# Interleaving two arrays on one core: one DMA queue in a fixed order and 64 KiB store rows, in place of two queues and a graded tail

## The chip, the core and the metric

The kernel runs on one core of a Trainium2 chip. The time is that of the device for one execution, in microseconds. Of the kernel before, five executions were timed: a median of 318.57 us, from 318.37 to 319.57. One more view of it is a profile of a single execution, which took 318.37 us; its span, from the first to the last instruction, is 316.2 us. The remaining 2.17 us lie around the span.

## The reference

Two arrays of 32 x 256 x 1024 single-precision numbers are interleaved element by element. Nothing is calculated; the task is moving 67.11 MB in and 67.11 MB out.

```python
def reference(x, y):
    batch, seq, dim = x.shape
    result = np.zeros((batch, seq, dim * 2), dtype=np.float32)
    result[..., 0::2] = x
    result[..., 1::2] = y
    return result
```

Since the last dimension is interleaved and the arrays are contiguous, the output is the flat x and the flat y interleaved, whatever the outer dimensions are. The kernel treats all three arrays as flat.

## The kernel before

The on-chip memory has 128 partitions. A tile takes a contiguous piece of the flat x and of the flat y and lays it over the 128 partitions, so many columns on each. The list `lwidths` (line 39) holds the widths in columns: seven tiles of 8192, then a graded tail of 4096, 2048, 1024, 512 and 512. A tile of 8192 columns is 4.19 MB of x and as much of y.

For each tile (loop at line 43) two loads are issued by SyncE's queue (SP): x at line 49, y at line 50. The pools `xp` and `yp` have two buffers each of 128 x 8192, so the loads of one tile can run while the one before is in use. The DMA engines' queue of SP appears as q1 in the profile.

Inside a tile an inner loop (line 53) takes up to 4096 columns at a time. For each piece VectorE (DVE) makes two copies into an output buffer `otile`, x into the even columns (line 63) and y into the odd ones (line 64), and ScalarE's queue (ACT) issues the store (line 65). The output pool `op` has two buffers of 128 x 8192. A store of a full piece writes a row of 32 KiB for each partition, 4.19 MB in all. The DMA queue of ACT appears as q10.

No order is written out by hand beyond this: SP issues the loads in the order of the tiles, ACT the stores in the order of the pieces, and each instruction waits for the semaphores that its buffers need. A load waits until the copy has read what was in its buffer two tiles earlier; the first copy of a piece waits until the store two pieces earlier has landed; a store waits for its second copy. Loads and stores of the two queues run on the same 16 DMA engines. All copies run on DVE; the other engines compute nothing.

Of the kernel before, what the change touches and what calls it, by code (L numbers as in the profile page):

```python
# [2 lines left out]

# [4 lines left out]


@with_exitstack
def kernel(
    ctx: ExitStack,
    tc: tile.TileContext,
    x: bass.AP,
    y: bass.AP,
    out: bass.AP,
):
    nc = tc.nc
    P = 128  # L20

    total = 1
    for s in x.shape:
        total *= s

    WL = 8192
    WS = 4096

    xf = x.rearrange("b s d -> (b s d)")
    yf = y.rearrange("b s d -> (b s d)")  # L30
    of = out.rearrange("b s d -> (b s d)")

    fp32 = mybir.dt.float32

    xpool = ctx.enter_context(tc.tile_pool(name="xp", bufs=2))
    ypool = ctx.enter_context(tc.tile_pool(name="yp", bufs=2))
    opool = ctx.enter_context(tc.tile_pool(name="op", bufs=2))

    lwidths = [WL] * (total // P // WL - 1) + [4096, 2048, 1024, 512, 512]
    assert sum(lwidths) == total // P  # L40

    start = 0
    for lw in lwidths:
        xtile = xpool.tile([P, WL], fp32, name="xtile")[:, :lw]
        ytile = ypool.tile([P, WL], fp32, name="ytile")[:, :lw]

        xs = dataclasses.replace(xf, offset=start, ap=[[lw, P], [1, lw]])
        ys = dataclasses.replace(yf, offset=start, ap=[[lw, P], [1, lw]])
        nc.sync.dma_start(out=xtile, in_=xs)  # L49
        nc.sync.dma_start(out=ytile, in_=ys)  # L50

        soff = 0
        while soff < lw:
            width = min(WS, lw - soff)
            otile = opool.tile([P, 2 * WS], fp32, name="otile")[:, : 2 * width]
            os_ = dataclasses.replace(
                of,
                offset=2 * start + 2 * soff,
                ap=[[2 * lw, P], [1, 2 * width]],
            )  # L60
            xsub = xtile[:, soff : soff + width]
            ysub = ytile[:, soff : soff + width]
            nc.vector.tensor_copy(out=otile[:, 0::2], in_=xsub)  # L63
            nc.vector.tensor_copy(out=otile[:, 1::2], in_=ysub)  # L64
            nc.scalar.dma_start(out=os_, in_=otile)
            soff += width

        start += P * lw
    assert start == total


# [1 line left out]
_INS = ['x', 'y']  # L73
_OUTS = [((32, 256, 2048), 'float32')]


# [23 lines left out]
```

## Time and profile before

| | |
|---|---|
| median of five executions | 318.57 us |
| profiled execution, whole | 318.37 us |
| its span | 316.2 us |
| bytes moved, in and out | 134.22 MB |
| mean rate over the span | 424 GB/s |
| copies on VectorE | 38, 73.5 us busy |
| one copy of 128 x 4096 | 2.295 us |
| loads of 4096 KB, from issue to landing (median) | x 43.6 us, y 60.8 us |
| stores of 4096 KB, from issue to landing (median) | 29.1 us |

A time from issue to landing includes the time that a transfer stands behind others in its queue. Of the profile's views, the slices show how full the 16 DMA engines are over the span, the queues show what each of the two queues moved, the chain follows the work that ended last back from the end, and the stretches give the DMA rate between any two moments. The rate by stretches counts a packet where it starts, so a stretch of a microsecond or two swings above and below the mean; stretches of a whole tile don't.

### The profile page before, as it was taken

What the parts mean: (1) busy time and instruction counts of PE and PEld (TensorE: products, weight loads), DVE (VectorE), ACT (ScalarE), POOL (GpSimd) and SP (SyncE); (2) the same over time, 40 slices, a digit from 0 to 9 for tenths busy, and PEclk for the clock granted to TensorE, in tenths of its full rate; (3) what the DMA queues carried; (4) which work ended last, traced back from release to release, by engine and by line L of the source; (5) the groups of instructions that cost most, each with busy time, mean ns of one, the idle gap of its engine ahead of it and who ended that gap; (6) DMA issues with size and microseconds to landing.
All of it is one profiled execution on the core that took longest, in us unless ns stands there. A gap on an engine that the chain in (4) does not pass through costs nothing.

```text
span 316.2 us, 179 instructions
## 1 busy us (share of the span) xinstructions
DVE 73.5 (23%) x38; POOL 0.2 (0%) x4
## 2 busy tenths in 40 slices
DVE  0334002232022410325003150130502223221022
POOL 0000000000000000000000000000000000000000
DMA  8999999999999999999999999999999999999997
GB/s 332 406 456 390 406 464 398 464 410 452 423 439 431 431 431 431 452 410 456 406 460 402 464 402 460 423 439 427 435 431 431 439 444 404 433 460 423 396 417 299
DMA packets 6192, 134.22 MB, mean 424 GB/s; under 512 B 688, under 2 KB 688, under 8 KB 1712
## 3 DMA queue, kind: packets, MB, share of 16 engines
q1 hardware_dynamic: 3456, 67.11, 49.9%
q10 hardware_dynamic: 2736, 67.11, 49.2%
HBM read 67.11 MB, written 67.11 MB: 424 GB/s over the span
## 4 chain that ended last, share of the span: by engine, by line
DMA 76%; DVE 11%; another core or an unknown queue 10%; issue 0%; DVEq 0%; SPq 0%
DMA out_dram<-otile 63%; DMA ytile<-in_y_dram 13%; DVE otile L64 6%; DVE otile L63 5%; DVEq L63 0%; SPq L49 0%
## 5 line engine op out<-in xcount | busy, mean ns | idle before, releaser
L63 DVE COPY otile<-xtile 128x4096 f32<-128x4096 f32 (+3 forms) x19 | 37.1, 1958 | 193.7 <-DMA out_dram<-otile 170.7
L64 DVE COPY otile<-ytile 128x4096 f32<-128x4096 f32 (+3 forms) x19 | 37.1, 1955 | 45.4 <-DMA ytile<-in_y_dram 45.4
L84 POOL MEMSET const-bfloat16-1.0<- 128x1 bf16 x1 | 0.1, 101 | 0.0
L84 POOL MEMSET const-uint8-127<- 128x1 uint8 x1 | 0.1, 101 | 0.0
L84 POOL MEMSET const-float32-0.0<- 128x1 f32 x1 | 0.1, 98 | 0.2 <-issue 0.2
L84 POOL MEMSET const-float32-1.0<- 128x1 f32 x1 | 0.1, 98 | 0.0
## 6 DMA issues: line engine op xcount, KB each, us to landing
out_dram<-otile ACTq DMA_DIRECT2D x15, 4096.0 KB, 29.1
xtile<-in_x_dram SPq DMA_DIRECT2D x7, 4096.0 KB, 43.6
ytile<-in_y_dram SPq DMA_DIRECT2D x7, 4096.0 KB, 60.8
xtile<-in_x_dram SPq DMA_DIRECT2D x1, 2048.0 KB, 38.8
ytile<-in_y_dram SPq DMA_DIRECT2D x1, 2048.0 KB, 51.2
out_dram<-otile ACTq DMA_DIRECT2D x1, 2048.0 KB, 7.7
xtile<-in_x_dram SPq DMA_DIRECT2D x1, 1024.0 KB, 29.8
ytile<-in_y_dram SPq DMA_DIRECT2D x1, 1024.0 KB, 36.1
```

What stands on the lines that cost most here:

```text
L63: nc.vector.tensor_copy(out=otile[:, 0::2], in_=xsub)
L64: nc.vector.tensor_copy(out=otile[:, 1::2], in_=ysub)
L84: nc = _bacc.Bacc("TRN2", target_bir_lowering=False, num_devices=1)
```

## The change

The tail is no longer graded: the kernel now runs eight tiles of 8192 columns. All DMAs, stores too, are issued from SyncE's queue, in an order that the program writes out: loads of tiles 0 and 1; then, for each tile t, its copies and its store, and after it the loads of tile t + 2. The output pool has one buffer of 128 x 16384 instead of two of 128 x 8192, and a tile's copies and its store cover all its columns at once, so a store writes a row of 64 KiB for each partition. Only the last tile is split in two halves of 4096 columns, and its output goes through the buffers of the x and y pools that tile 6 has left free.

The same on-chip memory is used: 192 KiB of each partition in both kernels (four input buffers of 32 KiB, and 64 KiB for output).

```diff
-    lwidths = [WL] * (total // P // WL - 1) + [4096, 2048, 1024, 512, 512]
-    opool = ctx.enter_context(tc.tile_pool(name="op", bufs=2))
+    opool = ctx.enter_context(tc.tile_pool(name="op", bufs=1))
...
-        nc.sync.dma_start(out=xtile, in_=xs)
-        nc.sync.dma_start(out=ytile, in_=ys)
...
-            nc.vector.tensor_copy(out=otile[:, 0::2], in_=xsub)
-            nc.vector.tensor_copy(out=otile[:, 1::2], in_=ysub)
-            nc.scalar.dma_start(out=os_, in_=otile)
...
+    def load(t):
+        if t >= n:
+            return
+        base = t * P * W
+        xt = xpool.tile([P, W], fp32, name="xtile")
+        yt = ypool.tile([P, W], fp32, name="ytile")
+        for tl, src in ((xt, xf), (yt, yf)):
+            s = dataclasses.replace(src, offset=base, ap=[[W, P], [1, W]])
+            nc.sync.dma_start(out=tl, in_=s)
+        tiles[t] = (xt, yt)
+
+    def emit(t, off, width, ot):
+        xt, yt = tiles[t]
+        nc.vector.tensor_copy(out=ot[:, 0::2], in_=xt[:, off : off + width])
+        nc.vector.tensor_copy(out=ot[:, 1::2], in_=yt[:, off : off + width])
+        d = dataclasses.replace(
+            of, offset=2 * (t * P * W + off), ap=[[2 * W, P], [1, 2 * width]]
+        )
+        nc.sync.dma_start(out=d, in_=ot)
+
+    load(0)
+    load(1)
+    for t in range(n):
+        if t < n - 1:
+            ot = opool.tile([P, 2 * S], fp32, name="otile")
+            emit(t, 0, S, ot)
+        else:
+            for i, pool in enumerate((xpool, ypool)):
+                ot = pool.tile([P, W], fp32, name="xtile" if i == 0 else "ytile")
+                emit(t, i * W // 2, W // 2, ot)
+        load(t + 2)
```

Here n is 8, P is 128, and W and S are both 8192.

More of the change, by code (lines that the diff above doesn't have):

```diff
@@ L20 @@
     P = 128
+    W = 8192
+    S = 8192
     total = 1
@@ L24 @@
         total *= s
-    WL = 8192
-    WS = 4096
+    n = total // (P * W)
+    assert n * P * W == total
     xf = x.rearrange("b s d -> (b s d)")
@@ L36 @@
     ypool = ctx.enter_context(tc.tile_pool(name="yp", bufs=2))
-    opool = ctx.enter_context(tc.tile_pool(name="op", bufs=2))
-    lwidths = [WL] * (total // P // WL - 1) + [4096, 2048, 1024, 512, 512]
[L40 to L64, printed above, removed]
-            nc.scalar.dma_start(out=os_, in_=otile)
-            soff += width
-        start += P * lw
@@ L69 @@
-    assert start == total
+    opool = ctx.enter_context(tc.tile_pool(name="op", bufs=1))
+    tiles = {}
+    def load(t):
[16 more added lines that the diff above has]
+        nc.sync.dma_start(out=d, in_=ot)
```

## The prediction

> **What bounds the kernel now.** I read the page first: engines, then DMA queues, then the chain of waits; then the DMA rate by stretches, because the chain alone misleads here.
>
> ```profile
> DVE 73.5 (23%) x38; POOL 0.2 (0%) x4
> DMA packets 6192, 134.22 MB, mean 424 GB/s; under 512 B 688, under 2 KB 688, under 8 KB 1712
> q1 hardware_dynamic: 3456, 67.11, 49.9%
> q10 hardware_dynamic: 2736, 67.11, 49.2%
> DMA out_dram<-otile 63%; DMA ytile<-in_y_dram 13%; DVE otile L64 6%; DVE otile L63 5%; DVEq L63 0%; SPq L49 0%
> ```
>
> VectorE (DVE) works 23% of the span. The two queues (q1 loads, q10 stores) together fill 99.1% of the 16 DMA engines' time. So the chain's "stores 63%" and the 170.7 us in which DVE waits for stores name who waits, not what is scarce: while one store is late, the engines are moving something else. A cure for those waits alone is worth nothing. The stretches show where the engines are not full:
>
> ```profile
> 0.00:20.00 20.00, 4.50 (x2) 0.20 (x4) 1.00 0.95 393
> 20.00:40.00 20.00, 4.50 (x2) 0.00 (x0) 1.00 1.00 415
> 40.00:58.57 18.57, 4.59 (x2) 0.00 (x0) 1.00 0.99 429
> 58.57:97.31 38.74, 9.09 (x4) 0.00 (x0) 1.00 1.00 433
> 97.31:136.02 38.71, 9.09 (x4) 0.00 (x0) 1.00 1.00 433
> ...
> 281.30:302.86 21.56, 3.84 (x4) 0.00 (x0) 1.00 1.00 421
> 302.86:311.70 8.84, 0.76 (x2) 0.00 (x0) 1.00 0.98 407
> 311.70:316.20 4.50, 0.84 (x2) 0.00 (x0) 1.00 0.54 220
> ```
>
> The last two columns are the engines' busy share and GB/s. In the middle one tile of 8192 columns (8.39 MB in, 8.39 MB out) takes 38.73 us, 433.3 GB/s, five times over (58.57 to 252.21). At that rate 134.22 MB need 309.76 us of the 316.2. The other 6.4 us, each as length x (1 - rate/433.3): start 1.86; 20 to 40, where the first store enters, 0.85; 40 to 58.57 about 0.18; the graded tail 0.61 + 0.54 + 2.2 = 3.35; the rest small. Only these can be won.
>
> The same rate with loads alone: the first two loads of 4.19 MB, one queue, are seen to land when their copies start.
>
> ```profile
> 0.73 0.37 SPq L49 DMA_DIRECT2D xtile<-in_x_dram  x1
> 1.15 0.42 SPq L50 DMA_DIRECT2D ytile<-in_y_dram  x1
> 13.10 4.50 DVE L63 COPY otile<-xtile 128x4096 f32<-128x4096 f32 x2 [13.10 <-DMA xtile<-in_x_dram]
> 22.78 4.50 DVE L64 COPY otile<-ytile 128x4096 f32<-128x4096 f32 x2 [5.18 <-DMA ytile<-in_y_dram]
> ```
>
> 22.78 - 13.10 = 9.68 us for 4.19 MB, again 433 GB/s, with a completion between the two loads.
>
> **What the Trainium skill says.** The page "DMA: Bandwidth & Descriptors" bears on it four times. "Where 436 GB/s comes from" gives a ceiling of 435.2 GB/s for the core's 16 ports; the trace's 433.3 lies 0.4% under it, so the middle has nothing to give. "Issuing engines are not separate DMA queues" says that transfers from all issuing engines share the same 16 engines, so a second queue adds no bandwidth; one queue at 433 (start) and two at 433 (middle) agree. "Queues, rings and completion order" says an engine takes one ring's descriptors in order without barriers, only the semaphore increment waits for earlier writes; the load-to-load boundary above agrees, a store-to-load boundary inside one ring is in no part of this trace. "Why a DMA increments its semaphore by 16 and not by 1" has one descriptor move one contiguous run and names rows *longer* than 64 KiB as those to be cut, so I expect a 64 KiB row to stay whole; the trace has only rows up to 32 KiB.
>
> **The change, part by part.**
>
> *Copies.* 38 copies become 14 of 8192 columns and 4 of 4096. The 8192 form is not shown; from the rows of 4096 (2295 ns) and 2048 (1228 ns) a column costs 0.52 ns, so it takes 2295 + 4096 x 0.52 = 4.43 us (between 4.43 and twice 2295, 4.59). A tile costs 8.9 us, as before (9.09).
>
> *Single output buffer.* Copies of tile t+1 now wait for the whole store t, then need 8.9 us before store t+1 can be issued. What covers this is the load pair of tile t+2, queued right behind store t: 2 x 9.68 = 19.4 us. Slack 10.5 us, less a completion and an issue (a store's shortest issue-to-landing was 2.6 us): still some 8. Cost nothing. Without the cover it would be 8.9 plus about 2 us for each of six tiles, 65 us.
>
> *One queue on SP.* Store t waits on SP for the second copy; behind it wait only the loads of tile t+2. They were issued after their own buffer's copy and now go out about 4.4 us later for x, and one issue (0.33 us) later for y. At store 0 that is 22.78 + 4.43 = 27.2 us; the second pair keeps the engines busy until 13.10 + 3 x 9.68 = 42.1. Afterwards each store is issued about 8 us before the load pair in front of it ends. Nobody starves. ACT's queue has nothing left; POOL's had nothing.
>
> *Order of directions.* Before, both queues always held work, so reads and writes alternated packet by packet. Now 8.39 MB of stores alternate with 8.39 MB of loads: seven entries into stores, six back. Unseen: pure-store rate, and a switch inside one ring. Nearest row: the first store, 0.85 us lost once. Later a direction changed at nearly every packet at no loss, so I take the 0.85 as the price of the first store, paid once, and 0 for the other twelve; bounds 0 and 0.85 each.
>
> *Rows of 64 KiB.* Half as many store packets. A 32 KiB packet takes 16 x 32768 B / 433.3 GB/s = 1.210 us, 5 ns above the ceiling's 1.205. Stores are 128 such packets per engine, and 7/8 of them are paired: between 0 and 0.3 us gained. I take the middle, 0.15.
>
> *Tail.* The five graded tiles go; tile 7 is full. Its load pair stands before store 6 in the queue, its four copies (4 x 2.3 us; the first needs only x) and both stores fall under store 6's 19.4 us. The engines stay full to the last packet, in rows of 32 KiB. Only the landing and the closing barrier remain: the last store before was issued at 312.7, landed 2.6 us later, 315.3; to the end 0.9 us.
>
> *Sum.* Lead of the first load, 13.10 - 9.68 = 3.42; data 309.76; first store 0.85; end 0.9: span 314.9, that is 1.3 us less. The profiled execution took 318.37, 2.17 beyond its span: 317.1. It lies 0.2 under the median of 318.57, so the sum stated for a median is 317.3; less the packets' 0.15, I predict 317.1. It is a gain of 0.46%; 0.2%, 0.64 us, is about what can be told from no change: under 317.9 is faster, over 319.2 slower.
>
> **Rivals.**
>
> *A: a switch costs each time (slower).* Each entry of a store behind a load in one ring costs what the first store cost, because no second ring fills the gap. For it: the 415 GB/s stretch is the only time a store began with no store before it. Against: packetwise alternation cost nothing later. Price 6 more x 0.85 = 5.1: 322.2. From (319.2 - 317.1) / 6 = 0.35 us per entry on, the kernel is slower.
>
> *B: stores alone run below loads alone.* For it: no pure-store stretch is seen. Against: q10's share for equal bytes is smaller (49.2 to 49.9%). At 425 GB/s the stores take 157.9 instead of 154.9 us: 320.1. Slower below 427.5.
>
> *C: a little of both, no change.* A completion's wait inside the ring, 0.1 us at each of 13 switches, gives 1.3 us: 318.4, between 317.9 and 319.2.
>
> *D: the tail's gain is whole and pure phases reach the ceiling.* First store free (0.85), and the stores' half of the data at 435.2 (0.7, the packets' gain within it) in place of the 0.15: 317.1 - 0.85 - 0.55 = 315.7 at best.
>
> **How the numbers follow.** Forecast, with its own range 316.2 to 317.9: 0.44; D below it 0.08; C 0.17; A 0.17; B 0.10; something unseen that lets the queue run dry 0.04. Faster 0.44 + 0.08 = 0.52; same 0.17; slower 0.31. The range leaves out about one in ten on each side: 315.9 cuts the end of D, 321.9 keeps A up to 0.8 us per entry and cuts its full price and the dry queue.
>
> **What would show it.** Right: copies of 4.4 us; each store issued before the load pair ahead of it ends; 433 GB/s in store stretches and across switches; full slices to the last; 128 packets a store besides the completions; span near 314.9. Wrong: a dip at each switch (A), stores of 8.39 MB spaced over 19.5 us (B), DVE's second copy ending after the load pair has landed (dry queue).

## The result: no difference that matters, and one late DMA engine

The changed kernel took 318.76 us (median of 43 executions, 317.05 to 319.66); the kernel before, beside it, 319.0 us (80 executions). The ratio is 0.9988, with a 95% interval of 0.9981 to 0.9995: the kernel is faster by 0.12%, where 0.46% was forecast. Its profiled execution took 319.21 us and has a span of 317.4, not 314.9. Beyond the span lie 1.78 us; in the kernel before it was 2.17.

The page of the changed kernel, its lines on engines, DMA packets, the queue, and the chain by line:

```profile
DVE 70.4 (22%) x18; POOL 0.2 (0%) x4
DMA packets 3600, 134.22 MB, mean 423 GB/s; under 512 B 400, under 2 KB 400, under 8 KB 400
q1 hardware_dynamic: 3600, 134.22, 98.4%
...
DMA out_dram<-otile 49%; DMA ytile<-in_y_dram 22%; DVE otile L56 8%; DVE otile L55 7%; DVE xtile L56 1%; DVEq L99 1%; SPq L50 0%; SPq L60 0%; DVEq L55 0%
```

3600 packets are 25 DMAs of 128 rows and 16 completions each, so a row of 64 KiB travels as one packet. The queue fills 98.4% of the engines' time; before, two queues filled 99.1%. Nothing on this page says what is wrong. The stretches do. The columns are again the busy share of the DMA engines and GB/s at the end of each line:

```profile
20.00:40.00 20.00, 4.43 (x1) 0.00 (x0) 1.00 0.99 419
62.62:101.50 38.88, 8.77 (x3) 0.00 (x0) 1.00 1.01 437
101.50:140.46 38.96, 8.77 (x3) 0.00 (x0) 1.00 1.00 432
140.46:179.83 39.37, 8.76 (x3) 0.00 (x0) 1.00 1.00 431
179.83:219.61 39.78, 8.76 (x2) 0.00 (x0) 1.00 1.00 433
...
297.30:311.00 13.70, 0.00 (x0) 0.00 (x0) 1.00 1.01 438
311.00:313.00 2.00, 0.00 (x0) 0.00 (x0) 1.00 0.83 360
313.00:315.00 2.00, 0.00 (x0) 0.00 (x0) 1.00 0.04 16
315.00:317.40 2.40, 0.00 (x0) 0.00 (x0) 1.00 0.03 14
```

The rate holds at 431 to 437 through every change of direction, as forecast. But a tile, bounded here by the moments when a whole store has landed, takes 38.9 us at first and up to 39.8, against 38.73. And the end is odd: from 313 to 317.4 the 16 engines are 3 to 4% busy. One sixteenth is 6%, so on average less than one engine is still at work there while all the others are done. Such an end is called a foot below.

The trace also records when each of the 16 engines has landed its share of a DMA. It doesn't name the engine, so first, median and last below are those of each DMA by itself. For the second load of some tiles and for the last store (us; the last column is the distance between the first and the last engine):

```
changed kernel                first    median   last     spread
y of tile 0                    22.05    22.42    22.68    0.63
y of tile 1                    42.26    42.61    43.04    0.79
y of tile 3                   119.72   120.15   120.91    1.19
y of tile 4                   158.43   158.88   160.39    1.96
y of tile 5                   197.13   197.62   200.21    3.08
y of tile 7                   274.54   275.05   277.90    3.36
last store                    313.17   313.67   316.64    3.46
```

The median engine ends at 313.67, a little ahead of the 314.0 that the prediction's sum implies (314.9 less 0.9). The last one ends 2.97 us later, and 2.2 of these separate it from the last but one. In the kernel before the spread is 0.4 to 0.6 us from the first large load to the last. The packets' durations show where the time is lost: every 64 KiB packet took 2.42 us, within 7 ns; most 32 KiB packets took 1.213 us; but after the beginning there are slow load packets, of 1.3 to 2.3 us, at 38 to 41, 80, 119, 157, 196, 235 and 274 us, always among the last two or three loads of an engine before its next store. At 38 to 41 this hits all engines (the price of the first store, expected); afterwards a few.

The copies and the queue are as forecast. The timeline of the changed kernel for one tile (start, duration):

```profile
62.62 4.43 DVE L55 COPY otile<-xtile 128x8192 f32<-128x8192 f32 x1 [35.49 <-DMA out_dram<-otile]
66.97 4.42 DVE L56 COPY otile<-ytile 128x8192 f32<-128x8192 f32 x1
71.42 0.34 SPq L60 DMA_DIRECT2D out_dram<-otile  x1
71.81 0.43 SPq L50 DMA_DIRECT2D xtile<-in_x_dram  x1
```

4.43 and 4.42 us a copy; the store is issued at 71.42, and the loads ahead of it land at 81.9, so 10 us of work stand before it.

### The profile page after: what moved, and what is told of

Its sections match the earlier page's. It is cut to its first block, busy times and chain, and to the rows that moved or that the text cites. A ratio compares the mean times of both kernels' runs of the same rounds, so it can differ in the third digit from the quotient of the medians.

```text
span 317.4 us, 100 instructions
## 1 busy us (share of the span) xinstructions
DVE 70.4 (22%) x18; POOL 0.2 (0%) x4
## 3 DMA queue, kind: packets, MB, share of 16 engines
q1 hardware_dynamic: 3600, 134.22, 98.4%
## 4 chain that ended last, share of the span: by engine, by line
DMA 71%; DVE 16%; DVEq 1%; SPq 0%; issue 0%
DMA out_dram<-otile 49%; DMA ytile<-in_y_dram 22%; DVE otile L56 8%; DVE otile L55 7%; DVE xtile L56 1%; DVEq L99 1%; SPq L50 0%; SPq L60 0%; DVEq L55 0%
## 5 line engine op out<-in xcount | busy, mean ns | idle before, releaser
L55 DVE COPY otile<-xtile 128x8192 f32<-128x8192 f32 x7 | 31.0, 4428 | 200.4 <-DMA out_dram<-otile 187.4
L56 DVE COPY otile<-ytile 128x8192 f32<-128x8192 f32 x7 | 31.0, 4422 | 5.3 <-DMA ytile<-in_y_dram 5.3
L56 DVE COPY xtile<-ytile 128x4096 f32<-128x4096 f32 x1 | 2.3, 2295 | 5.4 <-DMA ytile<-in_y_dram 5.4
L55 DVE COPY xtile<-xtile 128x4096 f32<-128x4096 f32 x1 | 2.3, 2295 | 0.9 <-DMA xtile<-in_x_dram 0.9
L56 DVE COPY ytile<-ytile 128x4096 f32<-128x4096 f32 x1 | 2.3, 2289 | 0.0
L55 DVE COPY ytile<-xtile 128x4096 f32<-128x4096 f32 x1 | 2.3, 2287 | 0.0
```

The costliest lines, as they stand in the source:

```text
L55: nc.vector.tensor_copy(out=ot[:, 0::2], in_=xt[:, off : off + width])
L56: nc.vector.tensor_copy(out=ot[:, 1::2], in_=yt[:, off : off + width])
```

## The experiments

Each time below is the median of its kernel, each ratio that to the kernel before on the same chip, with its 95% interval; a kernel without a ratio was timed in one execution. The theories named in the expectations are explained there; they call the part of a queue that one engine works off its ring.

**The changed kernel again, the row length, and the number of changes.** The first run repeats the changed kernel.

> The changed kernel once more, for a second profile. Theory DRIFT: in one ring each of the 16 DMA engines runs on its own; where loads give way to stores an engine that is behind still reads while the others write, its last load packets are slowed, and it stays behind to the end. Then one or a few engines again finish 2 to 3 us after the median one, with the loss made at the ends of load phases; span 316.5 to 317.6. Theory ACCIDENT: the late engine of the first profile was an event of that execution alone; then all engines finish within 1 us and the span is about 315.

318.0 us, ratio 0.9967 (0.9955 to 0.9978). The profile has a span of 317.1. In it the median engine ended at 314.02, the last at 316.30, 2.28 later; slow load packets before the stores at 156 to 158, 197, 236 and 274. So it was no accident, though here four engines were late by 0.8 to 2.3 us, not one. DRIFT's picture of where the time goes held. The foot differs between executions: this profile is of the slowest of 22 (316.66 to 318.88 us). An estimate: in the profiles that the table further down lists, the time is the landing of the last engine and 2.6 us; the median of 318.0 then puts the last engine at 315.4, 1.4 us behind the median engine.

Stores of half the size, two output buffers, one queue:

```diff
-    S = 8192
+    S = 4096
-    opool = ctx.enter_context(tc.tile_pool(name="op", bufs=1))
+    opool = ctx.enter_context(tc.tile_pool(name="op", bufs=2))
-            ot = opool.tile([P, 2 * S], fp32, name="otile")
-            emit(t, 0, S, ot)
+            for off in range(0, W, S):
+                ot = opool.tile([P, 2 * S], fp32, name="otile")
+                emit(t, off, S, ot)
```

> One queue as in the changed kernel, but stores of 4.19 MB with 32 KiB rows from two output buffers. DRIFT: the phases are the same (8.39 MB of loads, 8.39 MB of stores), so one engine drifts 2 to 3 us as well; time within 0.2% of the changed kernel. Theory LONG ROWS: the 64 KiB packets are what lets an engine fall behind; then the engines stay within 0.7 us and the time is near 317, 0.5% below the kernel before.

318.71 us, ratio 0.9986 (0.9973 to 0.9999); the last engine 2.31 us after the median. The rows of 64 KiB are out as a cause, and the single large output buffer with them.

Store halves and load halves in turn, on top of the edit above (`copies`, `store` and `load_one` are the parts of `emit` and `load`):

```diff
...
-            for off in range(0, W, S):
-                ot = opool.tile([P, 2 * S], fp32, name="otile")
-                emit(t, off, S, ot)
+            oa = opool.tile([P, 2 * S], fp32, name="otile")
+            copies(t, 0, S, oa)
+            ob = opool.tile([P, 2 * S], fp32, name="otile")
+            copies(t, S, S, ob)
+            store(t, 0, S, oa)
+            load_one(t + 2, 0)
+            store(t, S, S, ob)
+            load_one(t + 2, 1)
-        load(t + 2)
```

> One queue, 32 KiB rows, but store halves and load halves alternate: 4.19 MB stored, 4.19 MB loaded, and so on, so there are 13 changes from loads to stores in place of 7. DRIFT: twice as many changes, so the late engine is at least as late, 2 to 5 us, time 0 to 0.7% above the changed kernel. Theory PRICE PER SWITCH (every engine loses at each change): every engine loses, the median too, by up to 0.2 us at each. LONG ROWS: near 317.

320.77 us, ratio 1.0059 (1.0043 to 1.0074). The stretches of its end:

```profile
311.00:313.00 2.00, 0.00 (x0) 0.00 (x0) 1.00 0.83 360
313.00:315.00 2.00, 0.00 (x0) 0.00 (x0) 1.00 0.23 98
315.00:317.00 2.00, 0.00 (x0) 0.00 (x0) 1.00 0.11 49
317.00:318.90 1.90, 0.00 (x0) 0.00 (x0) 1.00 0.00 0
```

The same picture with a longer foot. The median engine ended at 313.77, as in the other kernels, the last at 318.12, 4.35 later. A price per switch that all engines pay is thereby refuted: 13 changes instead of 7 cost the median engine nothing. The time is 0.87% above that of the changed kernel on this chip, more than the 0.7% that DRIFT allowed.

**Two queues with the full tail.** Taken from the half-size kernel: stores on ScalarE's queue, with the exception of the second store of tile 6 and those of tile 7.

```diff
-    load(1)
...
+        load(t + 1)
...
-                emit(t, off, S, ot)
+                emit(t, off, S, ot, nc.sync if (t, off) == (n - 2, S) else nc.scalar)
...
-        load(t + 2)
```

> Two queues as in the kernel before (stores of 4.19 MB on ScalarE's queue), but the tail of the changed kernel: eight full tiles, the second store of tile 6 and those of tile 7 on SyncE's queue behind the last loads, tile 7 out through input buffers. DRIFT: reads and writes alternate packet by packet until tile 6, so the engines stay within 0.5 us, and the tail's gain shows: span about 314.8, time 317.0, 0.5% below the kernel before and 0.4% below the changed one. If the tail is what costs in the changed kernel, this one loses as well: 318.5 or more.

316.46 us, ratio 0.9926 (0.9912 to 0.9940), and span 314.8. This is faster than both kernels: 0.74% below the one before, and 0.5% below the changed one on the same chip (318.0). Its stretches, a tile in the middle and the end:

```profile
94.76:133.49 38.73, 9.09 (x4) 0.00 (x0) 1.00 1.00 433
...
284.94:311.00 26.06, 4.50 (x2) 0.00 (x0) 1.00 1.02 441
311.00:313.00 2.00, 0.00 (x0) 0.00 (x0) 1.00 0.64 279
313.00:314.80 1.80, 0.00 (x0) 0.00 (x0) 1.00 0.01 0
```

There is no foot: the engines stop together, 313.54 the median and 313.96 the last. The tail's gain is real, and the one queue had consumed it. Of the 2.4 us below the kernel before, 2.0 lie in the span (medians 316.7 and 314.7); the other 0.4 lie outside it, where all kernels derived from the changed one have about 1.8 us and the one before 2.2. Why that is stays open. A second profile of the same kernel:

> The kernel of two queues and full tail once more, for a second profile beside the changed kernel's three one-queue profiles. STEP (two rings keep the 16 engines in step): spread of a few packets at most that does not grow, last store's engines within 1.2 us; 316.3 to 317.0. ACCIDENT (its small spread was luck): an engine 2 us late at the end, 318 or more.

316.99 us, ratio 0.9939 (0.9921 to 0.9956), 313.56 and 313.91. In the middle of both profiles one engine was a packet out of step with the others, 1.3 to 1.4 us, and stayed so without losing more.

**Still smaller pieces.** Stores and loads of 2.1 MB in turn, in one queue, with four output buffers; taken from the kernel with halves in turn.

```diff
-    S = 4096
+    S = 2048
...
-            store(t, 0, S, oa)
-            load_one(t + 2, 0)
-            store(t, S, S, ob)
-            load_one(t + 2, 1)
+            for i in range(W // S):
+                store(t, i * S, S, os[i])
+                load_half(t + 2, i // 2, i % 2)
```

> One queue; stores of 2.1 MB and loads of 2.1 MB alternate, so 25 changes from loads to stores (7 in the changed kernel, 13 with halves). The last engine ended 2.3 to 3.0 us after the median one with 7 changes and 4.3 after it with 13. DRIFT PER CHANGE: the lag goes with the number of changes, some 6 to 9 us, while the median engine ends near 314; time 322 to 325. DRIFT FROM LONG PHASES: the lag comes of reading or writing for long without alternating and goes down as the pieces get smaller; then below 318. PRICE PER SWITCH: the median engine too is later than 315.

321.57 us, ratio 1.0085 (1.0071 to 1.0100). The two DRIFT theories don't fit. The last engine was 3.31 us behind the median, less than with 13 changes: the lag is not proportional to the number of changes, it had grown to that size by 212 us and then stood still. The sign of PRICE PER SWITCH did come: the median engine ended at 315.81, 2.04 us later than with halves. But the packets account for it: a row of 16 KiB took 0.611 us, 4.5 ns more than half of the 1.213 of a 32 KiB row, and 416 of them on each engine make 1.87 us. It is the shorter rows that cost here; the twelve further changes cost the median engine 0.2 us at most.

**Loads alone.** All stores but the last left out.

```diff
-        nc.sync.dma_start(out=d, in_=ot)
+        if t == n - 1 and off == W // 2:
+            nc.sync.dma_start(out=d, in_=ot)
```

> The changed kernel with all stores left out but the last (4.19 MB), so the copies are made and their output is mostly not written. One change from loads to stores, at the end. DRIFT PER CHANGE: the engines stay within 0.7 us through all 16 loads, each load 9.70 us after the one before; no load packets are slowed except the first and those just before the one store. DRIFT FROM LONG PHASES: the late engine shows with loads alone, by 1 us or more at the last load. Span about 3.4 + 154.9 + 9.7 + 0.8 + 0.9 = 169.7 plus the copies that stand before the store, some 7.

176.94 us, span 175.2. The 16 loads landed 9.71 us apart, with a spread of 0.63 to 0.66 us at every one, and after the first packets none took over 1.26 us. Loads by themselves make no engine late; stores are needed.

**Two queues with the single buffer.** The load pair that covers the copies, and for which the prediction priced the single output buffer at nothing, was to lose that part: the stores move to the other queue.

```diff
-        nc.sync.dma_start(out=d, in_=ot)
+        nc.scalar.dma_start(out=d, in_=ot)
```

> The changed kernel with its stores on ScalarE's queue, nothing else. The prediction said that the single output buffer costs nothing because the load pair behind each store covers the copies. With two queues that pair runs beside the store, not after it, so both end together and the 8.9 us of copies, with about 2 us of landing and issue, lie bare at each of 6 tiles: span 375 to 385. If the copies are covered anyway: 315 to 318.

336.1 us, 17.4 more than the kernel before on that chip (318.72), so the direction held and the price, a span of 375 to 385, was wrong by far. The 40 slices of its page:

```profile
GB/s 314 439 439 439 376 502 376 431 482 396 416 459 392 408 494 380 447 392 435 431 404 423 349 337 349 376 400 478 384 282 380 435 443 435 125 376 502 376 439 314
```

There are holes (337, 282, 125) in the second half alone; in the last of them no engine moves anything from 288 to 294 us. The load of x goes out as soon as its own copy ends, while earlier loads are still on their way, and so the two queues rarely run dry at once: part of the cover stayed. Here too the engines parted: landings of one DMA lay up to 14.5 us apart.

**An early small store.** The full-tail kernel with a first piece of 256 columns, whose store is issued at 3.6 us.

```diff
...
+    nc.sync.dma_start(out=hx, in_=dataclasses.replace(xf, offset=0, ap=[[H, P], [1, H]]))
+    nc.sync.dma_start(out=hy, in_=dataclasses.replace(yf, offset=0, ap=[[H, P], [1, H]]))
     load(0)
+    nc.vector.tensor_copy(out=ho[:, 0::2], in_=hx)
+    nc.vector.tensor_copy(out=ho[:, 1::2], in_=hy)
+    nc.scalar.dma_start(
+        out=dataclasses.replace(of, offset=0, ap=[[2 * H, P], [1, 2 * H]]), in_=ho
+    )
```

> The kernel of two queues and full tail, with a small piece of 256 columns loaded, copied and stored first, so that the first store is issued at about 5 us and not at 25. FIRST STORE ONCE: the slow load packets at 27 to 29 us move to the time of the small store, and the two slow beginnings overlap; up to 0.8 us less, 315.7 to 316.5. If the price belongs to the first large store, they stay at 27 and the time is that of the kernel without the head, 316.5, or 0.2 more for the small rows.

317.6 us, ratio 0.9958 (0.9944 to 0.9972), 0.6 to 1.1 us more than the two medians without the head. The stretch around the first large store, issued at 26.92:

```profile
10.00:26.00 16.00, 5.90 (x3) 0.00 (x0) 1.00 1.01 435
26.00:34.00 8.00, 3.09 (x2) 0.00 (x0) 1.00 0.99 381
```

381 against 433.3 over 8 us is 0.97 us lost. Counted by packets it is 0.86 us an engine: what the load packets between 28 and 32 us took beyond 1.213, divided by 16; without the head it was 0.71 and 0.79. The price stays at the first large store; it is no cost of the first store as such.

This run shows one thing more. The engines did not move in step: at most moments some read while others wrote. Yet the distance between the first and the last engine, 1.6 to 2.0 us, did not grow between 57 and 282 us.

**Stores that wait for the loads before them.** The first edit:

```diff
+        if t + 1 in tiles:
+            nc.vector.tensor_copy(out=ot[:, 1:2], in_=tiles[t + 1][1][:, 0:1])
+            nc.vector.tensor_copy(out=ot[:, 1:2], in_=yt[:, off : off + 1])
```

> The changed kernel, but each of the first seven stores is issued only when the pair of loads in front of it has landed on all engines (two extra copies of one column per tile carry the wait; the output is unchanged). So no engine still reads when a store is behind it in the ring or when another engine stores. Each of 7 changes then leaves the engines empty for about 2.3 us: time about 316.5 + 7 x 2.3 = 332.6. CHANGE (load packets lose time only near a change with stores behind or beside them): no slow load packets after the first, the engines within 0.7 us at every landing. CHANCE (single engines lose time at random, or at the ends of load phases whatever follows): lags of 1 us or more are still made in load phases, though each wait lets the late engine catch up.

322.27 us, ratio 1.0104 (1.0078 to 1.0130), and it isn't the kernel that the expectation describes. Its timeline shows why:

```profile
17.46 0.33 SPq L50 DMA_DIRECT2D xtile<-in_x_dram  x1
...
42.58 0.35 SPq L63 DMA_DIRECT2D out_dram<-otile  x1
42.97 0.43 SPq L50 DMA_DIRECT2D ytile<-in_y_dram  x1
```

The next x load was ordered ahead of the store, since its buffer came free earlier, so the engines never ran empty and a store still stood behind a load. The spread of the landings nevertheless stayed under 1.0 us. The run decides nothing; it does show that 7 changes need not bring a late engine.

With one instruction that frees both input buffers at the end:

```diff
+        if t + 1 in tiles:
+            nc.vector.tensor_copy(out=ot[:, 0:1], in_=tiles[t + 1][1][:, 0:1])
+            nc.vector.scalar_tensor_tensor(
+                out=ot[:, 0:1],
+                in0=yt[:, off : off + 1],
+                scalar=0.0,
+                in1=xt[:, off : off + 1],
+                op0=mybir.AluOpType.mult,
+                op1=mybir.AluOpType.add,
+            )
```

> What the run with two extra copies was meant to be: each of the first seven stores is issued only when the pair of loads in front of it has landed on all engines, and the next loads stay behind the store (two extra instructions of one column per tile, the output unchanged). The 16 engines run empty for about 2.3 us at each of 7 changes and start each store together: time 316.5 + 7 x 2.3 = 332.6. CHANGE: load packets lose time only where a store stands behind them or another engine stores beside them, so none is slow after the first loads, and every landing lies within 0.7 us over the engines. CHANCE: slow load packets and landings spread by 1 us or more are still there at the ends of load phases.

335.24 us; its timeline:

```profile
42.12 0.15 DVE L58 COPY otile<-ytile 128x1 f32<-128x1 f32 x1 [15.07 <-DMA ytile<-in_y_dram]
42.31 0.16 DVE L59 SCALAR_TENSOR_TENSOR otile<-ytile,xtile 128x1 f32<-128x1 f32 x1
42.50 0.35 SPq L70 DMA_DIRECT2D out_dram<-otile  x1
42.89 0.43 SPq L50 DMA_DIRECT2D xtile<-in_x_dram  x1
```

Now the store goes out after the loads have landed, and CHANGE held for the loads: no load packet before a store was slow, the spread was at most 0.73 us and 0.19 at the end. The time was 2.6 us more than the 332.6 expected. Slow packets now stood at the other change. At each of the six from a store to loads, the last 64 KiB packet of all 16 engines took 2.76 to 3.56 us in place of 2.42, and the first load after it was slow on 6 to 10 of them.

**Half of the engines late from the start.** One extra load of 8 partitions ahead of all others; its data is not used.

```diff
+    junk = opool.tile([P, 2 * S], fp32, name="otile")
+    j = dataclasses.replace(xf, offset=0, ap=[[W, 8], [1, W]])
+    nc.sync.dma_start(out=junk[0:8, :W], in_=j)
     load(0)
```

> The changed kernel with one extra load of 8 partitions (32 KiB rows, the data is not used) ahead of the first, which gives half of the engines one more packet of 1.21 us, so that they are about 1.2 us behind from the start. FEEDBACK: an engine that is behind still reads while the others store and loses more at each change, so the gap grows to 3 us or more by the end and the time is 319 or more. NO FEEDBACK: the late half stays 1.2 us behind at every landing; time about 316.5 + 1.2 plus what single engines lose as before (2 us): 317.7 to 320; whether the gap of the two halves grows is what tells the two apart, not the time.

320.86 us, ratio 1.0064 (1.0028 to 1.0101). The whole kernel began later than meant: its first large load landed at 16.32 us on the median engine, against 12.73 in the changed kernel, so the time says nothing of the gap. Between the means of the eight earlier and the eight later engines lay 0.99 us at the first large load, 0.99 still at 152 us, then 1.21 at 200, 1.67 at 239 and 1.69 at the last store, where the last engine was 2.2 us behind the first. Neither outcome came: the gap grew, but late and not to 3 us. The late half lost more than the early one; that being late is the cause isn't settled by it.

## Why the prediction was wrong

**What bounds the kernel: right, with a blind spot.** Bytes at 433.3 GB/s set the end of the median engine to within 0.5 us of 314.0 in every kernel of the table. (Five tiles in 193.64 us are 433.2 rather than 433.3; that is 0.07 us in the sum.) But a DMA is done when its last engine is, and the mean rate over 16 engines doesn't show one that falls behind. The last two columns are the profiled execution and the median of the kernel's executions; in all six profiles the execution ends 2.6 us after the last engine's landing.

```
kernel                        median engine    last engine    profiled    median
changed, first profile           313.67          316.64       319.21      318.76
changed, second profile          314.02          316.30       318.88      318.0
one queue, 32 KiB rows           313.81          316.12       318.72      318.71
one queue, halves in turn        313.77          318.12       320.71      320.77
two queues, full tail            313.54          313.96       316.55      316.46
the same, second profile         313.56          313.91       316.50      316.99
```

**The step that failed** is "the 0.85 as the price of the first store, paid once, and 0 for the other twelve". As a mean over the engines that zero was right: whole tiles at 431 to 437 GB/s. For the end it had to be the price of the last engine, and that was 2.97 us (2.28 in the second profile) beyond the median in place of 0. Both profiled executions were slower than the median of theirs, so in most executions it was less. With it the span comes out: 314.93, less 0.36 by which the median engine was early, less 0.11 at the end, plus 2.97, is 317.43. The time of the profiled execution is off by less, 2.1 us (319.21 against 317.1), because the 2.17 us beyond the span that the sum took over from the kernel before were 1.78; that was luck. The ground of the zero, that packets had alternated before at no loss, was the wrong row: it comes from two queues that both hold work. Counting how many of the 16 engines are in a load packet, every 0.3 us, in the kernel before (from 65.0 on) and in the full-tail kernel with the early store (from 100.0 on):

```
before        16   8   0   0   0   8  16  16  16  16  16  16  16   8   0   0   0
early store   10  13   8   5   6   3   7  11  10  13   9   5   5   3   7  11  11
```

In the first the engines change direction together, in the second they don't, and the spread of landings grows in neither. So it is not the common step that protects them. In one ring the spread did grow, in the changed kernel and in every variant of it that issues its stores behind unfinished loads, least in the one with the misplaced x load. Pieces of 8.39, 4.19 and 2.1 MB in one ring all had it; no run alternates row by row in one ring, so two rings and short turns are not told apart.

**Copies, single buffer, order: right.** 4.43 us were forecast and measured; the stores were issued 10 us ahead of need, 8 were forecast. The side remark, 65 us without the cover, is not shown: with the stores in the other queue 17.4 us were lost (19 to 20 against the two-queue kernels with the full tail and two output buffers), but part of the cover stayed, and no run took all of it away.

**First store: right in size.** The second load of tile 1 landed 10.47 us after the first on the median engine, 0.76 over the 9.71 of loads alone; 0.85 had been taken. It is paid by the last load packets ahead of the store.

**Rows: right in direction, too small in size.** They stay whole, 2.418 us for 64 KiB against 2 x 1.213, a gain of 8 ns; 56 such pairs on an engine make 0.45 us, where 0.15 was taken and 0.3 the bound. In the time it can't be told: the kernel with 32 KiB rows was 0.7 us slower than the changed one on the same chip, and the executions of both spread over 2 to 3 us.

**Tail: right.** All engines but the late ones work to the last packet; with two queues the tail gave the span of 314.8 us that the sum had, at 314.9, for one.

**Rivals.** A fell as it was put: no engine pays 0.85 at each change, and the median pays nothing. But it named the place, the entry of a store behind loads in one ring: there the late engine lost its 2.97 us, on average 0.5 at each of the six entries after the first. B fell, though its sign came: on the median engine a store landed 19.7 us after the loads ahead of it, 0.3 more than 19.4, but the load behind it came 9.4 us later, 0.3 less than 9.71, and the whole tile took 38.7 to 38.8. C came nearest, with 318.4, but by luck: the median engine lost nothing at completions.

**What stays open** is why load packets before a store are slow at times, and why on some engines. Shown: after the first packets never with loads alone, never where the store was not yet issued, and in all kernels that keep to one ring with stores behind unfinished loads. Not shown: that reads suffer because other engines write. One engine of the full-tail kernel read while the others wrote for most of the time and lost nothing, and with the early store several did.

## What to carry to other kernels

Where transfers bound a kernel, look at the slowest of the 16 engines and not at their mean: a foot of a few per cent of DMA share at the end, after the rate has held to the last moment, is one engine or a few that fell behind, and a gain of less than 1% can vanish in it. With two queues that both hold work the last engine ended 0.4 us behind the median here (0.9 with the early store); in the changed kernel, and in one ring with smaller pieces in turn, it ended 2.3 to 4.4 us behind. Take a good part of a change by itself: the tail alone, in two queues, is the version to keep, at 316.5 to 317.0 us.

## What the runs showed that was not expected

The first large store has a price, 0.7 to 0.9 us an engine by the packets, that a small early store doesn't remove; yet with half of the engines late it was absent (9.71 us between the loads of tile 1, against 10.47). When the engines had run empty before each store, the change from store to loads had a price that it has nowhere else: up to 1.1 us on a packet of 2.42. In both cases it is the packets close to the change that are slow.
